# The strip copies of branch B's values: 16 DMAs of 512 KB in the second head group instead of 32 of 256 KB over both

## The chip, the core and the metric

One NeuronCore of a Trainium2 chip runs the whole kernel. Its engines are TensorE (PE, with its weight loads as PEld), VectorE (DVE), ScalarE (ACT), GpSimd (POOL) and SyncE (SP); each takes its instructions strictly in the order of its own list and waits for others by semaphores. SP does nothing but issue DMAs; ACT and POOL issue some as well. The metric is the time of one execution in microseconds, as the median of several runs. The kernel before takes 2136.32 us (2136.04 to 2136.45 in three runs).

## The reference

One encoder layer on two sequences, 512 and 1024 tokens of width 1024, in float32. Branch A is grouped-query attention (8 query heads on 2 key/value heads), branch B is a neighbourhood attention with 8 heads on a token grid 64 wide; both are gated, merged and projected, and a squared-ReLU MLP follows.

```python
z = xn @ w_in
qa, ka, va, qb, kb, vb, ga, gb = jnp.split(z, idx, axis=-1)
...
o_a = _gqa_attention(qa, ka, va)
o_b = _neighbourhood_attention(qb, kb, vb, rpb)   # 8 rows x 16 columns around each token
merged = jax.nn.sigmoid(ga) * (o_a @ w_proj_a) + jax.nn.sigmoid(gb) * (o_b @ w_proj_b)
h = x + merged @ w_out
h = h + jnp.square(jax.nn.relu(rmsnorm(h) @ w_mlp_up)) @ w_mlp_down
```

The values vb of branch B are what the change is about: 1024 tokens x 8 heads x 64 numbers in the longer sequence.

## The kernel before

The two sequences ("trunks") go through `run` one after the other, the short one (512 tokens, `NB` = 1, names with 0) first, the long one (1024 tokens, `NB` = 2, names with 1) second. The MLP of both follows. Every float32 product is made of three matmuls on a high and a low part: `split` (lines 197 to 208) lets ACT cut the high part of a loaded weight tile (L199) and DVE the low part in two halves (L206). Loaded weights pass through three shared buffers (`rawp`), so a load also waits until the load three before it has been cut.

For each trunk `run` does this:

- **Twice, for the head groups g = 0 and 1 (line 538 on):** first the projections of a group, tile by tile of 128 tokens: the heads of branch A (`zs`), and, two tiles behind, the values of branch B for four of the eight heads (`values`, tiles `zvs`, weights `w_vs` from `raw_vs`). Each value tile is split into its high and low part side by side, 128 numbers a head, and written by ACT into the DRAM tensor `vd` (tokens x 8 heads x 128, L652). Then branch A's attention of the group: eight units in the long trunk (`units`, four heads by two blocks of 512 queries), each with eight rounds of transposes, high and low part (`pths`, `ptls`) and products; the gate projection of the branch fills PE's gaps. ACT writes each unit's result (`oads`) and each gate tile (`zgs`) to DRAM.
- **Branch B (line 918 on):** the query and key projection of two heads (`qkproj`: queries `pqbs`, L992 and L994; keys `pkbs`, L1013 and L1015), then units (h, j) of a head h and a strip j of 16 columns: scores (`sbs`), bias (`bms` from `rects`), softmax (`pbs`), a turn through DRAM (`tbs`, `bhs`), and the product with the strip of values `vss` (`obs`). The gate projection of branch B (weights `raw_gs1_3328_c`, c = 0 to 7) fills the gaps.

A strip j needs the values of 32 columns, and neighbouring strips overlap. In the long trunk the kernel therefore first copies `vd` inside DRAM into four strip stores `vst[0..3]` (L808, `vsts` in the profile), rows of a strip standing in the order in which `prep_v` (L950) then loads them for one head, 256 KB for a head and a strip. One copy takes every fourth grid row (index a) of one strip j: a source pattern of 4 x 32 runs and a target of 128 runs. Before the change each run holds the four heads of one group (2 KB), so a copy is 256 KB and there are 16 of them in each group's branch A, two at each unit. The short trunk has no strip stores; it loads straight from `vd` (L956).

The order of each engine's instructions is not the order of the source. A scheduler orders the whole program by its own estimates of when data will be there, and gives the DMAs of SP and ACT eight completion semaphores in turn: a DMA waits until the DMA that had its semaphore before is complete. So a copy in SP's list may wait for a gate or output write of ACT that has nothing else to do with it, and everything behind it in SP's list waits too.

Of the kernel before, what the change touches and what calls it, by code (L numbers as in the profile page):

```python
# [22 lines left out]
GRID_W = 64  # L23
# [38 lines left out]
def encoder(ctx: ExitStack, tc: tile.TileContext, xs, outs, w):  # L62
# [21 lines left out]
    def phase(name, bufs=2):  # L84
        return tc.tile_pool(name=name, bufs=bufs, reuse_waits="tile")
# [7 lines left out]
    def mm(name):  # L93
        return pmm.tile([P, 512], F32, tag="mm", name=name)

    def big(name):
        return pbig.tile([P, 1024], F32, tag="big", name=name)
# [73 lines left out]
    def bias_row(r):  # L171
        nc.sync.dma_start(biases[r], shifted[:, :, 7 - r : 23 - r, :])
# [246 lines left out]
    def run(tr, nxt, first):  # L419
        N, x, T, NT, NB = tr.N, tr.x, tr.T, tr.NT, tr.NB  # L420
# [4 lines left out]
        vd = dram.tile([T, 8, P], F32, name=f"vd{N}")  # L425
        vst = [dram.tile([rows // 4, 32, 4, 8, P], F32, name=f"vst{N}_{j}") for j in range(4)] if NB == 2 else None
# [38 lines left out]
        def finish_o(o, n, dst, pool, nm, parts=None):  # L465

            t = pool.tile([HD, 512], F32, tag="ot", name=f"ot_{nm}", bufs=1)
            if len(o.shape) == 3:

                tv = t[:, : 2 * n].rearrange("p (i q) -> p i q", i=2)  # L470
                nc.scalar.activation(tv, o[HD:P], AF.Copy)
                nc.vector.tensor_tensor(tv, o[0:HD], tv, op=ALU.add)  # L472
                o = tv[:, 1]
            else:
                nc.scalar.activation(t[:, :n], o[HD:P, :n], AF.Copy)
            if parts is not None:
                hi, lo, ps = parts
                b = pool.tile([P, n], F32, tag="os", name=f"os_{nm}", bufs=2)[ps, :n]
                nc.vector.tensor_tensor(b, o[0:HD, :n], t[:, :n], op=ALU.add)
                nc.scalar.activation(hi, b, AF.Copy)  # L480
                nc.vector.tensor_tensor(lo, b, hi.bitcast(F32), op=ALU.subtract)
                return
            b = pool.tile([HD, n], F32, tag="os", name=f"os_{nm}", bufs=2)
            nc.vector.tensor_tensor(b[:, :n], o[0:HD, :n], t[:, :n], op=ALU.add)
            put(dst, b[:, :n])
# [39 lines left out]
        def load_v(g, alloc, pin=False, hold=None):  # L525
            return load_cols(win, 1792 + 256 * g, 256, f"v{N}_{g}", alloc, pin, hold)

        early = {}
        for g in range(2):
# [230 lines left out]
            with phase(f"phA{N}_{g}") as ph:  # L760
                units = [(h, qb) for h in range(4) for qb in range(NB)]
                PP = {}

                def s_tile(u, j):
                    h, qb = u
                    nm = f"{N}_{g}_{h}_{qb}_{j}"
                    q0 = (qb * 4 + j) * P
                    lhs = qT[h % 2][:, h // 2, q0 : q0 + P]
                    s = big(f"s{nm}")[:, :T]
                    for kb in range(NB):  # L770
                        ks = slice(kb * 512, kb * 512 + 512)
                        nc.tensor.matmul(s[:, ks], lhs, kT[:, 0, ks], start=True, stop=False)
                        nc.tensor.matmul(s[:, ks], lhs, kT[:, 1, ks], start=False, stop=True)  # L773
                    nm_ = sml.tile([P, 1], F32, tag="nm", name=f"nm{nm}")
                    nc.vector.tensor_reduce(nm_, s, axis=AX.X, op=ALU.max, negate=True)  # L775
                    p = ph.tile([P, T], F32, tag="P", name=f"p{nm}", bufs=8)
                    l = sml.tile([P, 1], F32, tag="l", name=f"l{nm}")
                    nc.scalar.activation(p, s, AF.Exp, bias=nm_, accum_out=l)  # L778
                    rl = sml.tile([P, 1], F32, tag="rl", name=f"rl{nm}")
                    nc.vector.reciprocal(rl, l)  # L780
                    nc.gpsimd.tensor_scalar(p, p, rl, 1.0, op0=ALU.mult, op1=ALU.mult)  # L781
                    PP[u, j] = p

                o_of = {}

                def pv(u, kc, hi, lo):
                    h, qb = u
                    if kc == 0:
                        o_of[u] = mm(f"o{N}_{g}_{h}_{qb}")
                    o = o_of[u]  # L790
                    nc.tensor.matmul(o, vhl[:, kc, :], hi, start=(kc == 0), stop=False)
                    nc.tensor.matmul(o, vhl[:, kc, :], lo, start=False, stop=(kc == NT - 1))
                    if kc == NT - 1:
                        r0 = (g * 4 + h) * HD
                        finish_o(o, 512, oad[r0 : r0 + HD, qb * 512 : qb * 512 + 512], ph, f"A{N}_{g}_{h}_{qb}")

                for j in range(4):
                    s_tile(units[0], j)
                    fill.pull(2)
                queue = []  # L800
                LAG = 2
                for ui, u in enumerate(units):
                    h, qb = u
                    if NB == 2:
                        hs = slice(4 * g, 4 * g + 4)
                        for a in range(2 * (ui % 2), 2 * (ui % 2) + 2):
                            c0 = (0, 8, 24, 32)[ui // 2]
                            nc.sync.dma_start(  # L808
                                vst[ui // 2][:, :, a, hs, :].rearrange("k c h d -> k c (h d)"),
                                vd[:, hs, :].rearrange("(k a c) h d -> a k c (h d)", a=4, c=GRID_W)[a, :, c0 : c0 + 32],  # L810
                            )
                    if first:
                        bias_row(g * 4 + ui)
                        if g == 0 and ui == 1:
                            early["a"] = load_a(1)
                        if g == 0 and ui == 2:
                            early["v"] = load_v(1, slot)
                    nxt_u = units[ui + 1] if ui + 1 < len(units) else None
                    sdone = 0
                    for kc in range(NT):  # L820
                        pt = mm(f"pT{N}_{g}_{h}_{qb}_{kc}")
                        for j in range(4):
                            nc.tensor.transpose(  # L823
                                pt[:, j * P : (j + 1) * P], PP[u, j][:, kc * P : (kc + 1) * P], ident
                            )
                        hi = ph.tile([P, 512], F32R, tag="pth", name=f"pth{N}_{g}_{h}_{qb}_{kc}", bufs=3)
                        lo = ph.tile([P, 512], F32R, tag="ptl", name=f"ptl{N}_{g}_{h}_{qb}_{kc}", bufs=3)
                        nc.scalar.activation(hi, pt, AF.Copy)  # L828
                        nc.vector.tensor_tensor(lo, pt, hi.bitcast(F32), op=ALU.subtract)  # L829
                        queue.append((u, kc, hi, lo))  # L830
                        if nxt_u is not None:
                            while sdone < 4 and kc >= ((0, 1, 3, 4) if NB == 2 else (0, 0, 1, 2))[sdone]:
                                s_tile(nxt_u, sdone)
                                sdone += 1

                        fill.pull(1 if NB == 1 or kc % 4 < 3 else 0)
                        if len(queue) > LAG:
                            pv(*queue.pop(0))
                fill.drain()
                for item in queue:  # L840
                    pv(*item)
# [80 lines left out]
        with phase(f"phB{N}") as ph:  # L922
# [268 lines left out]
            for i in range(n + 4 - NB):  # L1191
# [9 lines left out]
                if i < n:  # L1201
# [4 lines left out]
                    h, j = units[i]  # L1206
# [702 lines left out]
    for i, tr in enumerate(trunks):  # L1909
        run(tr, trunks[i + 1] if i + 1 < len(trunks) else None, i == 0)  # L1910
# [66 lines left out]
```

## Time and profile before

| | us |
|---|---|
| median of three runs | 2136.32 (2136.04 to 2136.45) |
| the profiled execution | 2136.87 |
| its span, first to last instruction | 2135.0 |
| PE busy / PEld busy | 2099.9 / 1840.2 |
| DVE / ACT / POOL busy | 1483.2 / 1146.3 / 362.0 |
| PE's granted clock, mean over the span | 0.997 |
| copies of the first set, first to last issue | 452.2 to 586.1 |
| copies of the second set, first to last issue | 655.5 to 791.2 |

Columns of rows below: in a timeline, start and length in us, engine, line, operation, output<-inputs, shapes, count, and in brackets the idle time of the engine before it with what ended it. "SPq" and "ACTq" are DMA issues; their length is that of the issue, not of the transfer. Buffer numbers are left out of names, so `vsts<-vds` stands for all copies. In the list of waits the numbers are the total, the count and the longest. Times in the windows and timelines are counted from the span's first instruction. The long trunk's first branch A ends near 581, the second group's projections near 655, its branch A near 782, and branch B follows.

### The profile page before, as it was taken

The page shows a single profiled execution, that of the slowest core. Times are in us where ns is not written, and L with a number is a line of the kernel's source. Part 1 is how long each engine was busy: PE and PEld are TensorE (multiplying, and loading weights), DVE is VectorE, ACT ScalarE, POOL GpSimd, SP SyncE. Part 2 cuts the span into 40 slices and gives each one's busy share as a digit, 9 for nine tenths or more (in the row PEclk, how much of TensorE's full clock was granted, in tenths as well). Part 3 has the DMA queues.
Part 4 walks back from the last instruction along what each step waited for, and adds up shares of the span by engine and source line. Part 5 has one row for each costly group of instructions (what it writes and reads, how often), then busy time and mean ns, then how long its engine had stood idle before and what let it go on. Part 6 is the DMA issues. An engine that isn't in the chain of part 4 may idle for free.

```text
span 2135.0 us, 31762 instructions
## 1 busy us (share of the span) xinstructions
PE 2099.9 (98%) x10871; PEld 1840.2 (86%) x10871; DVE 1483.2 (69%) x2793; ACT 1146.3 (54%) x2487; POOL 362.0 (17%) x446
## 2 busy tenths in 40 slices
PE   9999999999989999999999999999999999999998
PEld 8888778988888888888888899999999988888887
DVE  6665786767647756787882877778777777759563
ACT  6664653767556645555531556556655643434352
POOL 2232310323233314442101200003000000000000
PEclk9999999999999999999999999999999999999999
DMA  6437557520133038876472666578445799688561
GB/s 192 133 99 212 148 165 254 184 89 29 59 111 107 25 97 245 244 219 196 153 246 103 203 196 193 162 249 210 158 146 158 259 351 344 215 276 282 166 203 64
DMA packets 340072, 381.31 MB, mean 179 GB/s; under 512 B 30911, under 2 KB 267079, under 8 KB 339911
## 3 DMA queue, kind: packets, MB, share of 16 engines
q1 hardware_dynamic: 301687, 313.99, 46.9%
q10 hardware_dynamic: 31072, 45.11, 6.0%
q0 software_dynamic: 7152, 20.19, 3.5%
q8 instruction: 86, 1.41, 0.3%
q14 instruction: 75, 0.61, 0.1%
HBM read 282.68 MB, written 105.71 MB: 182 GB/s over the span
## 4 chain that ended last, share of the span: by engine, by line
PE 53%; DVE 1%; issue 0%; ACT 0%; POOLq 0%; POOL 0%; ACTq 0%; DVEq 0%
PE dn L212 20%; PE ua L212 6%; PE ud L212 6%; PE uc L212 6%; PE ops L212 4%; PE ub L212 3%; PE ppbs L212 2%; PE ppas L212 2%; PE dnf L212 2%; PE pt L353 0%; PE obs L212 0%; PE gpss L212 0%; PE sbs L212 0%; PE ptbs L1126 0%; DVE A L1452 0%
## 5 line engine op out<-in xcount | busy, mean ns | idle before, releaser
L212 PE MATMUL dn<-wd,ah 128*128 128x512 f32 x1248 | 384.3, 389 | 0.0
L212 PEld LDWEIGHTS dn<-wd,ah 128*128 128x128 f32 x1248 | 234.2, 188 | 48.7
L212 PE MATMUL dn<-wd,al 128*128 128x512 f32 x624 | 242.8, 389 | 0.0
L1451 ACT ACTIVATE ah<-ar 128x512 fp32r<-128x512 f32 x168 | 104.4, 628 | 206.0 <-PE dn L212 186.7
L212 PE MATMUL gpss<-xs_0h,w_gs 128*128 128x512 f32 x512 | 188.7, 402 | 0.8 <-DVE ot_Bs L472 0.4
L1452 DVE TENSOR_TENSOR al<-ar,ah 128x512 fp32r<-128x512 f32 x168 | 114.4, 687 | 75.5 <-ACT ah L1451 67.9
L212 PE MATMUL ud<-B,A 128*128 128x384 f32 x768 | 143.6, 334 | 0.7 <-DVE c L1569 0.7
L212 PE MATMUL uc<-B,A 128*128 128x384 f32 x768 | 143.7, 334 | 0.0
L212 PE MATMUL ua<-B,A 128*128 128x384 f32 x768 | 138.8, 334 | 0.0
L212 PEld LDWEIGHTS dn<-wd,al 128*128 128x128 f32 x624 | 117.1, 188 | 24.2
L781 POOL TENSOR_SCALAR ps<-ps,rls 128x1024 f32<-128x1024 f32 (+1 forms) x96 | 96.8, 1010 | 226.4 <-DVE rls L780 201.0
L212 PEld LDWEIGHTS ud<-B,A 128*128 128x128 f32 x768 | 133.9, 188 | 1.1 <-DVE c L1569 1.1
L212 PEld LDWEIGHTS uc<-B,A 128*128 128x128 f32 x768 | 134.1, 188 | 0.2 <-ACT A L1451 0.2
L212 PEld LDWEIGHTS ua<-B,A 128*128 128x128 f32 x768 | 133.7, 188 | 0.2
L829 DVE TENSOR_TENSOR ptls<-pTs,pths 128x512 fp32r<-128x512 f32 x160 | 107.7, 686 | 37.3 <-ACT pths L828 36.3
L828 ACT ACTIVATE pths<-pTs 128x512 fp32r<-128x512 f32 x160 | 94.0, 597 | 73.4 <-PE pTs L823 71.3
L212 PE MATMUL ops<-wh_os,mgs 128*128 128x512 f32 x384 | 119.4, 390 | 0.0
L775 DVE TENSOR_REDUCE nms<-ss 128x1 f32<-128x1024 f32 (+1 forms) x96 | 99.9, 1041 | 25.6 <-PE ss L773 25.1
L212 PEld LDWEIGHTS gpss<-xs_0h,w_gs 128*128 128x128 f32 x512 | 96.3, 189 | 18.9 <-DVE w_gs L206 0.7
L778 ACT ACTIVATE ps<-ss,nms 128x1024 f32<-128x1024 f32 (+1 forms) x96 | 93.2, 972 | 23.4 <-DVE nms L775 20.6
L180 POOL TENSOR_TENSOR rs_f<-ms_f,mhalf 128x1 f32<-128x1 f32 x6 | 4.0, 667 | 590.7 <-DVE ms_f L176 590.7
L823 PEld LDWEIGHTS pTs<-ident,ps 128*128 128x128 f32 x640 | 77.7, 140 | 28.6 <-POOL ps L781 4.3
(287 smaller groups left out, 5152.4 us busy)
## 6 DMA issues: line engine op xcount, KB each, us to landing
ar<-ud SPq DMA_DIRECT2D x120, 512.0 KB
br<-in_w_mlp_down_dram SPq DMA_DIRECT2D x72, 512.0 KB
rawu<-in_w_mlp_up_dram SPq DMA_DIRECT2D x64, 512.0 KB
ud<-c ACTq DMA_DIRECT2D x128, 192.0 KB
raw_gs<-in_w_in_dram SPq DMA_DIRECT2D x32, 512.0 KB
ud<-cs SPq DMA_DIRECT2D x64, 192.0 KB
tbs<-pbs SPq DMA_DIRECT2D x24, 384.0 KB
bhs<-tbs SPq DMA_DIRECT2D x24, 384.0 KB
```

Of the source, the lines that this page charges most:

```text
L180: nc.gpsimd.tensor_tensor(r[:, :n], m[:, :n], mhalf[:, :n], op=ALU.pow)
L212: op = nc.tensor.matmul(out, a, b, **kw)
L775: nc.vector.tensor_reduce(nm_, s, axis=AX.X, op=ALU.max, negate=True)
L778: nc.scalar.activation(p, s, AF.Exp, bias=nm_, accum_out=l)
L781: nc.gpsimd.tensor_scalar(p, p, rl, 1.0, op0=ALU.mult, op1=ALU.mult)
L823: nc.tensor.transpose(pt[:, j * P : (j + 1) * P], PP[u, j][:, kc * P : (kc + 1) * P], ident)
L828: nc.scalar.activation(hi, pt, AF.Copy)
L829: nc.vector.tensor_tensor(lo, pt, hi.bitcast(F32), op=ALU.subtract)
L1451: nc.scalar.activation(hi, src, AF.Copy)
L1452: nc.vector.tensor_tensor(lo, src, hi.bitcast(F32), op=ALU.subtract)
```

## The change

The copies are issued in the second group's branch A alone, two at each unit as before, and each now takes all eight heads.

```diff
-                    if NB == 2:
-                        hs = slice(4 * g, 4 * g + 4)
+                    if NB == 2 and g == 1:
                         for a in range(2 * (ui % 2), 2 * (ui % 2) + 2):
                             c0 = (0, 8, 24, 32)[ui // 2]
                             nc.sync.dma_start(
-                                vst[ui // 2][:, :, a, hs, :].rearrange("k c h d -> k c (h d)"),
-                                vd[:, hs, :].rearrange("(k a c) h d -> a k c (h d)", a=4, c=GRID_W)[a, :, c0 : c0 + 32],
+                                vst[ui // 2][:, :, a].rearrange("k c h d -> k c (h d)"),
+                                vd.rearrange("(k a c) h d -> a k c (h d)", a=4, c=GRID_W)[a, :, c0 : c0 + 32],
                             )
```

Thirty-two copies of 256 KB become sixteen of 512 KB; the bytes are the same. The strips of heads 0 to 3 now depend on the second group's copies too. The scheduler orders the program anew, and three places of its lists differ in what follows. (The new file is one line shorter, so lines behind 804 count one less. Numbers at the end of a name are buffers.)

**SP, from the loads for the second group's projections on.** `rawkvs` are weights of that group's branch A, `raw_vs` its value weights, `rts` rotary tables, `raw_gs_2304` gate weights. Before:

```order
L510 DMA rawkvs_1_7022<-in_w_in_dram 128x8x64 x2
L808 DMA vsts_0_4661<-vds_4660 128x1x512 x4
L808 DMA vsts_1_4662<-vds_4660 128x1x512 x4
L808 DMA vsts_2_4663<-vds_4660 128x1x512 x4
L808 DMA vsts_3_4664<-vds_4660 128x1x512 x4
L245 DMA raw_vs_1_0_7031<-in_w_in_dram 128x4x256
L245 DMA raw_vs_1_4_7038<-in_w_in_dram 128x4x256
L708 DMA rts_1_0_7047<-in_rope_dram 128x128
```

After:

```order
L510 DMA rawkvs_1_7006<-in_w_in_dram 128x8x64 x2
L245 DMA raw_vs_1_0_7015<-in_w_in_dram 128x4x256
L245 DMA raw_vs_1_4_7022<-in_w_in_dram 128x4x256
L245 DMA raw_gs_2304_4_0_7603<-in_w_in_dram 128x8x128
L708 DMA rts_1_0_7031<-in_rope_dram 128x128
```

The sixteen copies of the first set stood between the two kinds of weights and are gone; the value weights follow at once. On ACT their two cuts (`wh_vs`, L199) moved with them, from behind the squares of the third tile (`sqs_1_2`) to ahead of those of the first.

**SP, at the second group's copies and the start of branch B.** `rects` are bias rectangles, `raw_gs_3328` the gate weights of branch B, `raw_bqs_1` and `raw_bks_1` the query and key weights of the second pair of heads. Before; the four strip loads of head 0 (`vss_0`, L950) stand seven rows above this piece, ahead of the second set:

```order
L245 DMA raw_gs_3328_0_0_9252<-in_w_in_dram 128x8x128
L808 DMA vsts_0_4661<-vds_4660 128x1x512 x4
L808 DMA vsts_1_4662<-vds_4660 128x1x512 x4
L808 DMA vsts_2_4663<-vds_4660 128x1x512 x4
L808 DMA vsts_3_4664<-vds_4660 128x1x512 x4
L942 DMA rects_0_9233<-biases 128x768
L245 DMA raw_gs_3328_1_0_9395<-in_w_in_dram 128x8x128
L942 DMA rects_1_9434<-biases 128x768
L1255 DMA zgs_1_4666<-sgs_3328_0_0_9454 128x512
L245 DMA raw_gs_3328_2_0_9540<-in_w_in_dram 128x8x128
L245 DMA raw_bqs_1_0_9592<-in_w_in_dram 128x8x128
L245 DMA raw_bks_1_0_9595<-in_w_in_dram 128x8x128
```

After:

```order
L807 DMA vsts_0_4661<-vds_4660 128x1x1024 x4
L807 DMA vsts_1_4662<-vds_4660 128x1x1024 x4
L807 DMA vsts_2_4663<-vds_4660 128x1x1024 x4
L807 DMA vsts_3_4664<-vds_4660 128x1x1024 x4
L941 DMA rects_0_9217<-biases 128x768
L949 DMA vss_0_9219<-vsts_0_4661 128x4x128
L949 DMA vss_0_9219<-vsts_1_4662 128x4x128
L949 DMA vss_0_9219<-vsts_2_4663 128x4x128
L949 DMA vss_0_9219<-vsts_3_4664 128x4x128
L245 DMA raw_gs_3328_1_0_9379<-in_w_in_dram 128x8x128
L941 DMA rects_1_9418<-biases 128x768
L245 DMA raw_gs_3328_2_0_9524<-in_w_in_dram 128x8x128
```

The strip loads of head 0 now stand behind all sixteen copies, and the gate weights of columns 1 and 2 behind the strip loads. The semaphores tie the copies to other DMAs: copies 3, 4, 7, 9 and 11 (counted 1 to 16) wait for output writes (`oads`) of units 2, 5, 6, 7 and 8 of this group; copies 5, 8 and 10 for gate writes (`zgs`), 10 for the last of the group; copies 6 and 12 to 16 for the copies 3 to 8. The strip load of strip 0 waits for copy 10, that of strip 1 for 11, of strip 2 for 12, of strip 3 for 13 to 16.

**ACT, at the start of branch B.** `oads_4667<-os_As_1_3_1` is the last output write of branch A, `qBs` and `kBs` the query and key parts of the first pair of heads, by blocks of 512 tokens (`pqbs_0_0` the first, `pqbs_0_1` the second). Before:

```order
L435 DMA oads_4667<-os_As_1_3_1_9224 64x512
L992 ACTIVATE qBs_0_9258<-pqbs_0_0_9261 64x4x128 x2
L1013 ACTIVATE kBs_0_0_9259<-pkbs_0_0_9296 64x512 x2
L1013 ACTIVATE kBs_0_1_9260<-pkbs_0_0_9296 64x512
L992 ACTIVATE qBs_0_9258<-pqbs_0_1_9328 64x4x128 x2
L1013 ACTIVATE kBs_0_0_9259<-pkbs_0_1_9363 64x512 x2
```

After:

```order
L435 DMA oads_4667<-os_As_1_3_1_9208 64x512
L199 ACTIVATE w_bqs_0_9226<-raw_bqs_0_0_9224 128x1024
L199 ACTIVATE w_bks_0_9232<-raw_bks_0_0_9230 128x1024
L199 ACTIVATE w_gs_3328_0_9238<-raw_gs_3328_0_0_9236 128x1024
L991 ACTIVATE qBs_0_9242<-pqbs_0_0_9245 64x4x128 x2
L1012 ACTIVATE kBs_0_0_9243<-pkbs_0_0_9280 64x512 x2
L1012 ACTIVATE kBs_0_1_9244<-pkbs_0_0_9280 64x512
L199 ACTIVATE w_gs_3328_1_9381<-raw_gs_3328_1_0_9379 128x1024
L199 ACTIVATE w_gs_3328_2_9526<-raw_gs_3328_2_0_9524 128x1024
L991 ACTIVATE qBs_0_9242<-pqbs_0_1_9312 64x4x128 x2
L1012 ACTIVATE kBs_0_0_9243<-pkbs_0_1_9347 64x512 x2
```

The cuts of the first query, key and gate weights came from the midst of branch A to here, and the cuts of gate weights 1 and 2 from behind the first softmax operations to ahead of the second block's queries and keys. DVE's low parts moved along with them.

On PE the only moves are six swaps of a score matmul with the transposes next to it, and the first matmul of the fourth tile's projection, which went some 25 instructions later.

## Prediction

> **What bounds the kernel now.** I read the page first, then PE's waits, the windows, and the timelines of the two stretches that the change touches.
>
> ```profile
> span 2135.0 us, 31762 instructions
> PE 2099.9 (98%) x10871; PEld 1840.2 (86%) x10871; DVE 1483.2 (69%) x2793; ACT 1146.3 (54%) x2487; POOL 362.0 (17%) x446
> GB/s 192 133 99 212 148 165 254 184 89 29 59 111 107 25 97 245 244 219 196 153 246 103 203 196 193 162 249 210 158 146 158 259 351 344 215 276 282 166 203 64
> ```
>
> TensorE is busy for 2099.9 of 2135.0 us, so only some 35 us are waits. A change that moves DMAs can win back a few of these, or add new ones; it removes no matmul. PE's waits, as total, count and longest, name what there is to win:
>
> ```profile
> PE zvs L212 <- ACT wh_vs L199: 5.7, 1, 5.7
> PE sbs L212 <- DVE kBs L1015: 2.3, 2, 1.8
> ```
>
> The longest single wait of the program, 5.7 us, is at the first value matmul (zvs) of the long trunk's second group, for the weights that ACT cuts (wh_vs). The timelines of SP, ACT and PE there show why:
>
> ```profile
> 583.19 3.69 SPq L808 DMA_DIRECT2D vsts<-vds  x4
> 586.99 4.00 SPq L245 DMA_DIRECT2D raw_vs<-in_w_in_dram  x2
> ```
>
> ```profile
> 598.32 1.06 ACT L199 ACTIVATE wh_vs<-raw_vs 128x1024 fp32r<-128x1024 f32 x1 [3.29 <-DMA raw_vs<-in_w_in_dram]
> 599.61 1.06 ACT L199 ACTIVATE wh_vs<-raw_vs 128x1024 fp32r<-128x1024 f32 x1 [0.24 <-DMA raw_vs<-in_w_in_dram]
> ```
>
> ```profile
> 593.35 0.34 PE L212 MATMUL zs<-wghs,xs_0l 128*128 128x384 f32 x1
> 599.43 0.58 PE L212 MATMUL zvs<-wh_vs,xs_0h 128*128 128x256 f32 x1 [5.74 <-ACT wh_vs L199]
> 600.15 0.58 PE L212 MATMUL zvs<-wl_vs,xs_0h 128*128 128x256 f32 x1
> ```
>
> SP issues the value weights only at 586.99, behind the last four copies of the first set, and they land at 598.3, though ACT has been free for 3.3 us. The windows price what follows (columns: stretch, length, busy time of PE, PEld, DVE, ACT and POOL, granted clock, share of the 16 DMA engines, GB/s):
>
> ```profile
> 778.00:781.00 3.00, 3.00 (x17) 2.47 (x16) 1.38 (x2) 1.10 (x2) 0.64 (x1) 1.00 0.26 101
> 598.40:605.20 6.80, 5.33 (x22) 4.82 (x23) 5.28 (x8) 2.67 (x5) 2.96 (x4) 0.50 0.22 64
> ```
>
> From 598.4 to 605.2 the clock is 0.50: the idle stretch is paid a second time. The other row is a stretch in which the copies run with little else: 101 GB/s at a DMA share of 0.26, about four engines of 16. That is why 586.99 became 598.3: four copies of 256 KB at 101 GB/s take 10.4 us, and whatever is queued behind them on those engines waits.
>
> **Part 1, the first group's copies go: a gain.** SP's order after the change has the value weights straight behind the group's other weight loads, and ACT's order has both wh_vs cuts right after the last output write of branch A, ahead of the squares of three tiles. Their buffers are free long before, so the 5.74 us wait goes. So does what it caused: work from 599.4 to 605.2 at half clock, 5.8 us, costs 2.9 us, and a wait of 0.4 us for the low part (wl_vs) that follows in the same stretch is counted in my sum as well. **Gain 9.1 us** (5.74 + 0.44 + 2.9). Bounds: 5.7 if the clock fell for another reason, 9.1 at most. What is late next there? The rotated heads (rrs), which ACT now makes behind 2.1 us of cuts; they have the matmuls of the second and third tile as cover. From here everything in the second group's branch A runs 9.1 us earlier.
>
> **Part 2, cuts moved to the start of branch B: a loss, but a covered one.** The cuts of the query, key and gate weights now stand on ACT behind the last output write of branch A, where before they were done in its midst.
>
> ```profile
> 781.98 0.33 ACTq L435 DMA_DIRECT2D zgs<-sgs  x1
> 782.35 0.59 ACT L475 ACTIVATE ot_As<-os 64x512 f32<-64x512 f32 x1 [0.40 <-PE os L792]
> 783.69 0.46 ACTq L435 DMA_DIRECT2D oads<-os_As  x1
> ```
>
> ```profile
> 782.06 0.39 PE L212 MATMUL pqbs<-xs_0h,w_bqs 128*128 128x512 f32 x1
> 782.29 0.39 PE L212 MATMUL pqbs<-xs_0l,w_bqs 128*128 128x512 f32 x1
> ```
>
> PE starts the query projection at 782.06 now. After the change ACT is free for the cut only at 784.15 (783.69 + 0.46), cuts for 1.05 us, and the low half follows on DVE for 0.86 (both rows below): 786.1, where the second matmul, which needs it, ran at 782.29. That is 3.8 us of waiting, and half as much again of cold clock by the proportion of part 1 (5.74 us of waiting, 2.9 of cold clock) is 1.9. By itself 5.7 us. Part 3 comes later on the same path and swallows it.
>
> **Part 3, sixteen copies of 512 KB in one group: the large term.** Each copy takes one of eight completion counters shared by SP and ACT and waits for the DMA that used that counter before. The waits of SP between 640 and 860 us show it:
>
> ```profile
> SPq L808 <- DMA zgs<-sgs: 112.2, 5, 59.1
> SPq L808 <- DMA oads<-os_As: 14.2, 2, 9.3
> ```
>
> So the copies don't run ahead through the group's 130 us: they are paced by ACT's writes of gates and head outputs. In the changed order copy 9 follows the output write before the last, copy 10 the group's last gate write (zgs, issued at 781.98), copy 11 the last output write, and 12 to 16 only earlier copies. When does the last gate write release SP?
>
> ```profile
> 789.35 3.00 SPq L808 DMA_DIRECT2D vsts<-vds  x4
> 792.47 0.48 SPq L942 DMA_DIRECT2D rects<-biases  x1
> 793.06 2.07 SPq L245 DMA_DIRECT2D raw_gs<-in_w_in_dram  x1
> ```
>
> At 789.35, where copy 13 of before waited for the same write (7.4 us after its issue; the mask's load runs beside it). Four copies of 256 KB are left then. After the change **seven copies of 512 KB** are left, 3.67 MB instead of 1.05.
>
> A 512 KB copy has no row. Its two patterns keep their outer counts, 4 on the source and 128 on the target, and only the run grows from 2 to 4 KB; so I take the rate of the 101 GB/s row: 5.2 us each. Bounds: 1.3 us if all 16 engines took part (four times the rate), 6.2 us if sharing costs a fifth.
>
> By the Trainium skill, DMA: Bandwidth & Descriptors, section "Why a DMA increments its semaphore by 16 and not by 1", a DMA runs on the largest number of engines up to 16 that divides both outer counts, here still 4. The same page's section "Anatomy of one DMA" gives 2.0 us plus bytes at 436 GB/s, an estimate of 1.2 us of moving per copy; by that the sum would be the first rival's below. The share of 0.26 speaks against it here.
>
> What waits for them: all four strip loads of head 0 (vss) now read what these copies write, and the last of them stands in SP's queue behind copies 13 to 16. Behind it stand the gate weights of columns 1 and 2, and on ACT the cuts of these two now stand *ahead* of the second half of the query and key projection, which the first score matmul of branch B needs. Before, ACT had this:
>
> ```profile
> 804.02 1.19 ACT L1013 ACTIVATE kBs<-pkbs 64x512 fp32r<-64x512 f32 x2 [3.31 <-PE pkbs L212]
> ```
>
> ```profile
> 799.20 0.88 DVE L994 SCALAR_TENSOR_TENSOR qBs<-pqbs,qBs 64x128 fp32r<-64x128 f32 x4 [2.10 <-ACT qBs L992]
> 800.74 0.92 DVE L994 SCALAR_TENSOR_TENSOR qBs<-pqbs,qBs 64x128 fp32r<-64x128 f32 x4 [0.66 <-ACT qBs L992]
> 805.24 1.38 DVE L1015 TENSOR_TENSOR kBs<-pkbs,kBs 64x512 fp32r<-64x512 f32 x2 [3.58 <-ACT kBs L1013]
> ```
>
> ```profile
> 806.68 0.80 PE L212 MATMUL sbs<-kBs,qBs 128*128 128x384 f32 x3 [0.48 <-DVE kBs L1015]
> ```
>
> The path step by step, in the changed kernel's time:
> - Copy 10 issued: 789.35 - 9.1 = 780.25.
> - Seven copies: 36.3 us, and 2.0 us from issue to landing (the row pair below): 818.5.
> - Last strip load, gate weights 1, bias rectangle and gate weights 2 (256 + 512 + 384 + 512 KB) at 351 GB/s, the best slice of the page: 4.8 us, and 2.0 to landing: 825.3.
> - ACT cuts gate weights 2, 1.05; DVE's two low halves, 2 x 0.86: 828.0.
> - Query halves, 799.20 to 801.66 before: 2.5; key halves: ACT 1.19, DVE 1.38, with some 0.9 overlapped: **832.2**.
>
> ```profile
> 767.83 0.33 ACTq L435 DMA_DIRECT2D zgs<-sgs  x1
> 769.86 0.58 SPq L808 DMA_DIRECT2D vsts<-vds  x1
> ```
>
> ```profile
> L199 ACT ACTIVATE w_gs<-raw_gs 128x1024 fp32r<-128x1024 f32 x2 | 2.1, 1051 | 0.0
> L206 DVE TENSOR_TENSOR w_gs<-raw_gs,w_gs 128x512 fp32r<-128x512 f32 x4 | 3.3, 857 | 0.8 <-ACT w_gs L199 0.8
> ```
>
> The score matmul that ran at 806.7 runs at 832.2: 25.5 us later, the gain of part 1 already taken off. PE stands idle there for some 29 us (from 803.3, 806.7 - 9.1 + 5.7) with nothing else in its order, and restarts with a cold clock: by the row of part 1, 5.8 us at half, 2.9 us. I add 3.2, a little over it, as this wait is longer. **Net +28.7 us.** By the Trainium skill, TensorE: Matmul & The Clock Gate, section "What's actually happening", one busy window of about 3.4 us lifts the throttle; the restart would then cost 1.7 us, and the sum be 27.2. The 6.8 us of the row decide for me.
>
> Other moves cost nothing by these covers: score matmuls swapped with transposes in branch A (bounds -0.4 to +0.4 us each, the small waits of such places), merge operands (zas) asked for earlier, and the odd head's key copies on POOL behind four bias additions; they have the four units of head 0 as cover, 1 or 2 us if that is gone.
>
> **The sum.** The profiled execution took 2136.87 us, 1.87 around its span and 0.55 over the median of 2136.32. 2136.3 + 28.7 = **2165.0 us** for the median.
>
> **Rivals.**
> - *The copies drain in time.* If they use all engines, 1.3 us each, the chain ends at 805.0, PE gets there at 803.3, and the net is -1.7 us plus up to 1.7 of cold clock: about 2135. Below some 1.0 us a copy the chain is no longer late; there the net is -9.1 + 5.7 = -3.4, 2132.9. For it: 16 issues fewer and runs of twice the length. Against it: the share of 0.26.
> - *Eight engines, 2.6 us each.* The chain ends at 814.1: +7.4 + 2.9, 2146.6. Nothing in the rows points there.
> - *A second wait behind the first.* SP's queue then holds a weight load that waits for DVE ahead of the first softmax stores; if the first output matmul of branch B waits as well, 5 to 12 us more: about 2174.
>
> **How the numbers follow.** Forecast (2155 to 2172) 0.78; first rival 0.10, second 0.04, third 0.08. Within the forecast: 5 us less if the last gate write lands as fast as the earlier one (2.0 us), 3 less without a cold clock, 6 more at 6.2 us a copy. Range 2150 to 2177. Faster or slower means by over 0.2% (4.3 us), about what can be told from no change: faster 0.03, same 0.08, slower 0.89.
>
> **What would show it.** Right: no wait at zvs in the second group and clock 1.00 there; the copies at a DMA share near 0.25 for some 36 us after branch A; gate weights 1 issued some 38 us after copy 10; a PE wait of 25 to 35 us at sbs, put down to kBs. Wrong: copies on all engines; copies 4 to 9 issued much earlier than the writes that pace them; a different ACT operation ahead of the query halves.

## The result, and the profile after

| | before | changed |
|---|---|---|
| median, us (lowest to highest) | 2136.18 (2135.86 to 2136.45) | 2168.45 (2166.51 to 2170.15) |
| the profiled execution, us | 2136.87 | 2166.51 |
| its span, us | 2135.0 | 2164.6 |

The changed kernel is slower by a factor of 1.0151 (95% interval 1.0133 to 1.0168), 32.3 us between the medians. Its profiled execution is the shortest of its four, 29.6 us longer in span than the one before; the rows below explain these 29.6 us.

The page of the changed kernel, and under it its list of PE's waits (total, count, longest):

```profile
span 2164.6 us, 31745 instructions
PE 2100.9 (97%) x10871; PEld 1841.5 (85%) x10871; DVE 1481.8 (68%) x2793; ACT 1148.1 (53%) x2487; POOL 364.0 (17%) x446
```

```profile
PE sbs L212 <- ACT kBs L1012: 32.4, 1, 32.4
PE pqbs L212 <- ACT w_bqs L199: 3.1, 1, 3.1
```

PE is busy for about as long as before (2100.9 against 2099.9 us): no work was added, and 28.6 of the 29.6 us are waiting. The 5.7 us wait at zvs is gone from the list; two waits at the start of branch B have come. SP's timeline shows what holds them:

```profile
782.96 19.38 SPq L807 DMA_DIRECT2D vsts<-vds  x7
802.45 4.68 SPq L941 DMA_DIRECT2D rects<-biases  x1
807.17 13.65 SPq L949 DMA_DIRECT2D vss<-vsts  x4
820.92 0.52 SPq L245 DMA_DIRECT2D raw_gs<-in_w_in_dram  x1
821.48 1.42 SPq L941 DMA_DIRECT2D rects<-biases  x1
823.00 0.38 SPq L245 DMA_DIRECT2D raw_gs<-in_w_in_dram  x1
```

Seven copies are issued from 782.96 on, when the last gate write lets the tenth go. Even their issue stretches over 19 us, and the gate weights follow 38.0 us later. ACT's and PE's timelines carry it on:

```profile
826.35 1.06 ACT L199 ACTIVATE w_gs<-raw_gs 128x1024 fp32r<-128x1024 f32 x1 [33.88 <-DMA raw_gs<-in_w_in_dram]
829.27 1.06 ACT L199 ACTIVATE w_gs<-raw_gs 128x1024 fp32r<-128x1024 f32 x1 [1.87 <-DMA raw_gs<-in_w_in_dram]
830.35 0.59 ACT L991 ACTIVATE qBs<-pqbs 64x512 fp32r<-64x512 f32 x1
```

```profile
834.46 0.69 PE L212 MATMUL sbs<-kBs,qBs 128*128 128x384 f32 x1 [32.35 <-ACT kBs L1012]
```

ACT stood 33.88 us in front of a cut of gate weights, and the query halves (qBs) that PE needed stood behind it in ACT's order. The windows of the changed kernel (stretch, length, busy PE, PEld, DVE, ACT, POOL, granted clock, DMA share, GB/s), first while the seven copies run, then behind the two waits, and last the stretch that was at half clock before:

```profile
784.00:807.00 23.00, 18.11 (x80) 14.64 (x79) 3.85 (x11) 2.75 (x5) 0.00 (x0) 1.00 0.25 101
```

```profile
776.70:779.50 2.80, 2.80 (x7) 2.17 (x8) 2.80 (x5) 1.83 (x2) 0.00 (x0) 0.50 0.61 190
834.50:840.90 6.40, 5.67 (x14) 4.40 (x15) 4.66 (x11) 2.89 (x6) 1.77 (x3) 0.50 1.16 287
598.40:605.20 6.80, 6.80 (x50) 6.80 (x49) 4.36 (x11) 4.13 (x19) 1.67 (x3) 1.00 0.15 52
```

The copies move 101 GB/s at a quarter of the DMA engines, as before. Where PE starts again after these two waits it runs at half clock, for 2.8 and 6.4 us, and half of that is lost. From 598.4 to 605.2 the clock is now full.

### The profile page after: what moved, and what is told of

The parts are those of the page before. It is cut to its first block, busy times and chain, and to the rows that moved or that the text cites. A ratio compares the mean times of both kernels' runs of the same rounds, so it can differ in the third digit from the quotient of the medians.

```text
span 2164.6 us, 31745 instructions
## 1 busy us (share of the span) xinstructions
PE 2100.9 (97%) x10871; PEld 1841.5 (85%) x10871; DVE 1481.8 (68%) x2793; ACT 1148.1 (53%) x2487; POOL 364.0 (17%) x446
## 4 chain that ended last, share of the span: by engine, by line
PE 52%; DVE 1%; issue 0%; ACT 0%; POOLq 0%; POOL 0%; ACTq 0%; DVEq 0%
PE dn L212 19%; PE ua L212 6%; PE ud L212 6%; PE uc L212 6%; PE ops L212 4%; PE ub L212 3%; PE ppbs L212 2%; PE ppas L212 2%; PE dnf L212 2%; PE pt L353 0%; PE obs L212 0%; PE gpss L212 0%; PE sbs L212 0%; PE ptbs L1125 0%; DVE A L1451 0%
```

## The experiments

The theory: time is lost only as the copies that stand behind the last gate write are many and slow. Each takes its bytes at 101 GB/s, because its pattern has 4 as the outer count. The rivals: the rate of a DRAM-to-DRAM copy does not depend on the pattern; the size of one copy hurts; the pacing by ACT's writes hurts whatever the rate; the gain in the first group came from elsewhere.

### half: the same orders, half the bytes

```diff
-vst[ui // 2][:, :, a].rearrange("k c h d -> k c (h d)"),
-vd.rearrange("(k a c) h d -> a k c (h d)", a=4, c=GRID_W)[a, :, c0 : c0 + 32],
+vst[ui // 2][:, :, a, 4:8].rearrange("k c h d -> k c (h d)"),
+vd[:, 4:8].rearrange("(k a c) h d -> a k c (h d)", a=4, c=GRID_W)[a, :, c0 : c0 + 32],
...
-vst[j][:, :, :, h, :].rearrange("k c a d -> (c a) k d")
+vst[j][:, :, :, 4 + h % 4, :].rearrange("k c a d -> (c a) k d")
```

> The changed kernel with copies of 256 KB: the sixteen copies carry heads 4 to 7 only, and the strips of heads 0 to 3 are loaded from those of heads 4 to 7. Every engine's order is that of the changed kernel. Theory (seven copies stand ahead of the last strip load, and each takes its bytes at about 101 GB/s): 2.6 us a copy instead of 5.2, so the chain after the last gate write is 18 us shorter; the wait at the first score matmul of branch B falls from 32.4 to about 14 us, and the time from 2168.5 to about 2150 (2145 to 2152, the lower end if the last gate write also lands sooner). Rival A (the wait is for the gate write that paces the copies, or for their number, not their bytes): no change, 2167 to 2170. Rival B (a second wait behind the first fills what is won): 2160 or more.

Measured: 2140.57 us, ratio to before 1.0019 (1.0010 to 1.0028). The direction is the theory's, the size is not: 28 us less, where 18 were forecast. SP's timeline and PE's waits of this run:

```profile
781.17 2.53 SPq L807 DMA_DIRECT2D vsts<-vds  x4
783.82 1.71 SPq L941 DMA_DIRECT2D rects<-biases  x1
785.57 8.87 SPq L949 DMA_DIRECT2D vss<-vsts  x4
794.53 0.49 SPq L245 DMA_DIRECT2D raw_gs<-in_w_in_dram  x1
```

```profile
PE sbs L212 <- ACT kBs L1012: 4.1, 1, 4.1
PE pqbs L212 <- ACT w_bqs L199: 3.4, 1, 3.4
```

Only four copies are left behind the gate write here, not seven: the scheduler tied the semaphores differently although every engine's order is the same (perhaps because it expects a smaller copy to be done sooner; the runs don't show why). Four copies of 2.6 us are 10.4 us, and the gate weights are issued 13.4 us after the first of them. So the rule fits with the number of copies that this kernel really leaves behind; the expectation had carried the seven over. Rival B falls, and so does the part of A by which the pacing alone makes the wait. Number and bytes went down together here, so the run does not part them cleanly; but four copies of 5.2 us would be 20.8 us, more than the 13.4 that all of it took.

### wide and tiny: the pattern, and the floor

```diff
-vst[ui // 2][:, :, a].rearrange("k c h d -> k c (h d)"),
-vd.rearrange("(k a c) h d -> a k c (h d)", a=4, c=GRID_W)[a, :, c0 : c0 + 32],
+vst[ui // 2][:, :, a].rearrange("k c h d -> c k (h d)"),
+vd.rearrange("(k a c) h d -> a c k (h d)", a=4, c=GRID_W)[a, c0 : c0 + 32],
```

In tiny the pattern is the old one, with `4:5` in the place of `4:8` in the diff of half, and all strips are loaded from head 4.

> The changed kernel with the same sixteen copies of 512 KB, their patterns turned so that the outer dimension is the 32 grid columns on both sides instead of 4 and 128. Theory (the outer count of 4 holds a copy to four of the 16 engines): about 1.3 us a copy, a DMA share of 0.8 or more while they run, the seven copies done in some 10 us, no wait over 5 us at the first score matmul. The scheduler also moves the cuts of the query weights back into branch A here, so the 3.1 us wait at the query projection goes as well: 2127 us (2124 to 2133). Rival A (a copy from DRAM to DRAM runs at about 100 GB/s whatever its pattern): the long wait stays, 2160 to 2166. Rival B (eight engines): 2140 to 2146.

> The changed kernel with copies of 64 KB in the old pattern (4 outside): only head 4 is copied, and all strips are loaded from it. Every engine's order is that of the run wide. Theory: 0.65 us a copy on four engines, so the copies are out of the way, and this is the floor for wide: 2127 us (2124 to 2131), within 3 us of wide. If wide is much longer than this, the copies themselves still cost there; if both stay near 2168, the bytes of the copies are not what is waited for.

Measured: wide 2127.47 us, ratio to before 0.9957 (0.9942 to 0.9972); tiny 2126.83, 0.9954 (0.9939 to 0.9969). SP's row with all sixteen copies of wide, and a window in which they run with few other DMAs:

```profile
646.18 63.30 SPq L807 DMA_DIRECT2D vsts<-vds  x16
```

```profile
658.00:662.00 4.00, 4.00 (x22) 3.24 (x21) 2.65 (x5) 4.00 (x8) 0.72 (x2) 1.00 1.03 394
```

The same bytes, the same 4 KB runs: 394 GB/s at a share of 1.03, where the old order of the dimensions gave 101 at 0.25. This is the best stretch; from 650 to 660 it is 332 GB/s at 1.01. So the share is four times the old one, and the rate three to four times. (The share is a mean over the 16 engines; the trace does not tell them apart.) The rule of the Trainium skill weighed in the prediction (DMA: Bandwidth & Descriptors, "Why a DMA increments its semaphore by 16 and not by 1") agrees at both points: 4 engines for an outer count of 4, 16 for 32.

With tiny, an eighth of the bytes in the old pattern, the time is the same within the spread of either, so in wide the copies cost nothing any more. But the rate is not all that changed. The scheduler ties none of the sixteen to the last gate write here, nor in tiny: all are issued between 646 and 710, while the changed kernel issues the last seven from 782.96 on. The expected seven copies behind the gate write, done in 10 us, never came about, and how much of the gain is rate and how much is place these two runs do not tell. **wide beats both kernels**, by 9.1 us against the kernel before on its chip (2136.53).

### before_wide, wide_g0, wide_g1: where the first group's 9 us come from

The kernel before, in both groups (before_wide), for g == 0 alone (wide_g0) and for g == 1 alone (wide_g1):

```diff
-vst[ui // 2][:, :, a, hs, :].rearrange("k c h d -> k c (h d)"),
-vd[:, hs, :].rearrange("(k a c) h d -> a k c (h d)", a=4, c=GRID_W)[a, :, c0 : c0 + 32],
+vst[ui // 2][:, :, a, hs, :].rearrange("k c h d -> c k (h d)"),
+vd[:, hs, :].rearrange("(k a c) h d -> a c k (h d)", a=4, c=GRID_W)[a, c0 : c0 + 32],
```

> The kernel before, with its 32 copies of 256 KB in both groups, their patterns turned to 32 outside as in wide. Theory: the first set's last four copies take 2.6 us together instead of 10.4, the value weights behind them land some 8 us sooner, the 5.7 us wait at the first value matmul of the second group and the half clock behind it go: 2127 us (2125 to 2131). Rival (that wait has another cause, or the copies' rate does not depend on the pattern): 2135 to 2137.

> The kernel before with the turned pattern (32 outside) for the first group's sixteen copies alone; the second group's copies keep the old pattern and their order. Theory (all of the 9 us come from the value weights that queue behind the first set): no wait at the first value matmul of the second group, full clock there, 2127.5 us (2125.5 to 2129.5), as in the run before_wide. Rival (part of the 9 us came from the second group, for example from strip loads that land sooner): 2129.5 to 2134.

> The mirror of wide_g0: the turned pattern for the second group's copies alone. Theory (at branch B of the kernel before, PE waited only 0.5 us at the first scores, so faster copies have nothing to win there): the 5.7 us wait and the half clock stay, 2135.5 us (2134 to 2137). Rival of wide_g0: 2129 to 2134.

| run | median, us | ratio to before (95% interval) |
|---|---|---|
| before_wide | 2127.53 | 0.9957 (0.9941 to 0.9974) |
| wide_g0 | 2127.81 | 0.9957 (0.9941 to 0.9973) |
| wide_g1 | 2135.43 | 0.9994 (0.9984 to 1.0003) |

All three times came out as forecast. The whole gain comes from the first group: with the new pattern in its sixteen copies alone the 9 us are there. Faster copies in the second group alone give nothing, since before PE waited 0.5 us there. The way to the gain was another than forecast, though. Expected were four last copies that take 2.6 us in place of 10.4, and value weights that land some 8 us sooner. SP's timeline of wide_g0:

```profile
452.42 13.77 SPq L808 DMA_DIRECT2D vsts<-vds  x16
485.78 51.50 SPq L245 DMA_DIRECT2D raw_vs<-in_w_in_dram  x2
```

All sixteen are issued within 14 us, where before they took 134.65 us (452.22 to 586.87): none is held up by ACT's late writes any more. The value weights are issued 50 to 100 us sooner, and ACT cuts them at 583.44 without a wait for a DMA. before_wide shows the same. So it is shown that the 9 us go when the value weights no longer stand behind late copies; whether the rate alone would have done it, with the copies as late as before, is not. The longest waits of wide_g0 and wide_g1, one row of each list:

```profile
PE ss L772 <- ACT kTs L626: 2.5, 3, 1.2
```

```profile
PE zvs L212 <- ACT wh_vs L199: 6.1, 1, 6.1
```

In wide_g0 no single wait over 2 us is left in this list; in wide_g1 the wait for the value weights stays (6.1 us).

### last7_wide and first9_wide: rate and place apart

The edit of wide, in last7_wide only where this holds, in first9_wide only where it doesn't:

```diff
+2 * ui + a % 2 >= 9
```

> The changed kernel with the turned pattern (32 outside) for the copies 10 to 16 alone, those behind the last gate write. Every engine's order and every copy's semaphore wait are those of the changed kernel; only the rate of these seven differs. Theory (their rate alone makes the long wait): 1.3 us a copy instead of 5.2, 9 us in all instead of 36, so gate weights 1 are issued some 12 us after copy 10 (38 in the changed kernel), and the wait at the first scores falls from 32.4 to 1 to 5 us; the 3.1 us wait at the query projection and its cold clock stay: 2137 us (2132 to 2142). Rival A (the pacing by ACT's writes is the cause, whatever the rate): 2160 or more. Rival B (the copies 1 to 9 are still draining in front of them): 2145 to 2155.

> The mirror: the turned pattern for the copies 1 to 9, the old one for 10 to 16. Every engine's order is that of the changed kernel, but the scheduler ties the copies to other semaphores: copy 16 waits for the gate write before the last (some 760 us), no copy for the last one. Seven copies still run on four engines, 5.2 us each. Theory (a slow copy costs nothing if it is not left behind the last gate write): all copies done by some 780 us, no long wait at the first scores (under 4 us), the 3.1 us wait at the query projection stays: 2133 us (2130 to 2140). Rival (slow copies cost as such): 2145 to 2168.

Measured: last7_wide 2143.93 us, ratio 1.0032 (1.0020 to 1.0043); first9_wide 2130.86, 0.9973 (0.9961 to 0.9985). In last7_wide orders and semaphores are those of the changed kernel, and the rate of seven copies alone takes 24.5 us off. SP's timeline, a window while the seven run, and PE's waits:

```profile
782.71 5.14 SPq L807 DMA_DIRECT2D vsts<-vds  x7
...
798.63 0.45 SPq L245 DMA_DIRECT2D raw_gs<-in_w_in_dram  x1
```

```profile
788.00:796.00 8.00, 8.00 (x37) 6.64 (x36) 2.06 (x3) 1.78 (x3) 0.00 (x0) 1.00 0.99 307
```

```profile
PE sbs L212 <- ACT kBs L1012: 9.5, 1, 9.5
PE pqbs L212 <- ACT w_bqs L199: 3.1, 1, 3.1
```

The gate weights are issued 15.9 us behind the tenth copy (12 forecast, 38.0 in the changed kernel). The DMA share is 0.99, but the window, in which bias rectangles and strip loads run among the copies, has 307 GB/s, not 394; at that rate a copy is 1.7 us. So the wait is 9.5 us and not 1 to 5, and the time 2 us above the range that was forecast. Rival A falls. Rival B does not quite: the tenth copy goes at 782.71, as in the changed kernel, but from 779 to 783, before it is under way, the share is 0.25 to 0.29 at 82 to 99 GB/s, so an earlier copy of the old pattern is still running. What that adds to the 9.5 us was not tried.

first9_wide is the other half: seven copies run in the old pattern, but the scheduler ties none of them to the last gate write. A window while some of them run, and two rows of SP, the last copy and the first strip loads behind it:

```profile
664.00:672.00 8.00, 8.00 (x49) 6.79 (x48) 6.32 (x10) 4.64 (x9) 2.25 (x2) 1.00 0.25 103
```

```profile
764.92 0.58 SPq L807 DMA_DIRECT2D vsts<-vds  x1
...
778.25 1.03 SPq L949 DMA_DIRECT2D vss<-vsts  x2
```

They are as slow as ever (103 GB/s at 0.25), and cost nothing: the last is issued at 764.92, 18 us ahead of the changed kernel's tenth, and PE's wait at the first scores is 0.5 us. The 3.1 us wait at the query projection is left; with its cold clock it is more than the 3.4 us by which this run is above wide. **A slow copy is not what hurts, but a slow copy left behind the last gate write with SP's loads in its queue.**

### pieces: 32 copies of 256 KB in the second group

```diff
-nc.sync.dma_start(
-    vst[ui // 2][:, :, a].rearrange("k c h d -> k c (h d)"),
-    vd.rearrange("(k a c) h d -> a k c (h d)", a=4, c=GRID_W)[a, :, c0 : c0 + 32],
-)
+for hs in (slice(0, 4), slice(4, 8)):
+    nc.sync.dma_start(
+        vst[ui // 2][:, :, a, hs, :].rearrange("k c h d -> k c (h d)"), vd[:, hs, :].rearrange("(k a c) h d -> a k c (h d)", a=4, c=GRID_W)[a, :, c0 : c0 + 32],
+    )
```

> The changed kernel with its sixteen copies cut into 32 of 256 KB, all in the second group's branch A, old pattern: the place is changed, the size is that of before. By the scheduler's semaphores the 25th copy is the one that waits for the last gate write, so eight copies of 2.6 us (2.1 MB) stand behind it, where the changed kernel had seven of 5.2 us (3.7 MB). Theory (bytes behind the last gate write at 101 GB/s): 21 us of copies, first scores some 16 us sooner than in the changed kernel, a wait there of 14 to 20 us: 2150 us (2144 to 2156). Rival A (the size of one copy is what hurts): 2127 to 2137. Rival B (all bytes being in one group hurts, however they are cut): 2165 to 2172.

Measured: 2176.28 us, ratio 1.0183 (1.0167 to 1.0199): a miss by 20 us over the range. SP's and ACT's timelines:

```profile
791.78 10.60 SPq L808 DMA_DIRECT2D vsts<-vds  x8
802.49 4.36 SPq L941 DMA_DIRECT2D rects<-biases  x1
806.89 6.84 SPq L949 DMA_DIRECT2D vss<-vsts  x4
813.84 2.15 SPq L245 DMA_DIRECT2D raw_bqs<-in_w_in_dram  x1
```

```profile
820.89 1.06 ACT L199 ACTIVATE w_bqs<-raw_bqs 128x1024 fp32r<-128x1024 f32 x1 [35.47 <-DMA raw_bqs<-in_w_in_dram]
```

The chain of copies is what was forecast: eight of them, and the last strip load of head 0 is through SP 22.0 us after the first of the eight was issued. What failed is who stands behind it. In this order the query weights (raw_bqs) do too, which branch B needs first of all; the expectation had reckoned with the gate weights alone. PE waits 37.3 us at the query projection. The eight start 8.8 us later than the seven of the changed kernel as well (3.3 us of it is a new wait of PE in the second group's projections). Rival A (the size of one copy) falls: no copy of 512 KB is needed for the harm. Rival B (all bytes in one group) is not parted from the theory, since the order changed too, and its range of 2165 to 2172 lies nearer to what came out.

### pool_queue: the copies from another queue

```diff
-                            nc.sync.dma_start(
+                            nc.gpsimd.dma_start(
```

> The changed kernel with its sixteen copies (512 KB, old pattern, same place) issued from POOL's queue instead of SP's, two after each unit's softmax: they share no semaphore with ACT's gate and output writes, and nothing of SP's stands behind them. The scheduler reorders branch A's scores and transposes around them, so a few us either way belong to that. Theory (a slow copy does harm only as far as the pacing leaves it behind the last gate write, with SP's loads queued after it): the copies are done soon after 780 us, no wait over 6 us at the first scores, 2130 us (2125 to 2138). Rival (the copies' total time on four engines is the limit, or POOL's issue of them delays the softmax): 2145 or more.

Measured: 2149.17 us, ratio 1.0055 (1.0039 to 1.0071). Its list of DMA issues (KB each, median us from issue to landing) and PE's waits in the stretch:

```profile
vsts<-vds POOLq DMA_DIRECT2D x16, 512.0 KB, 8.7
```

```profile
PE ss L772 <- ACT ps L778: 9.3, 11, 2.7
PE os L791 <- ACT pths L827: 2.8, 4, 1.0
PE os L792 <- DVE ptls L828: 1.9, 5, 1.1
PE sbs L212 <- DVE kBs L1014: 0.5, 1, 0.5
```

The copies are still slow, 8.7 us to landing. At the first scores PE waits 0.5 us, as the theory said; but 14 us of small waits have come in branch A, and the time lies in the range of the rival. Whether the other order of scores and transposes makes these waits, or POOL's issue of the copies, was not parted. Inconclusive for the price, in line with the theory at the one place it was for.

### The waits add up

Each run's profiled execution against that of before_wide (2126.89 us), which has none of these waits; cold clock is half of the stretch at 0.50 behind each wait, by the window rows of that run. The rows that aren't above are these, of half, last7_wide and first9_wide:

```profile
776.80:782.80 6.00, 6.00 (x14) 4.75 (x15) 3.65 (x6) 1.81 (x2) 0.00 (x0) 0.50 0.18 53
807.80:813.60 5.80, 5.08 (x12) 4.00 (x13) 4.67 (x11) 2.89 (x6) 1.37 (x3) 0.50 1.20 290
```

```profile
777.00:780.30 3.30, 3.30 (x8) 2.58 (x9) 3.30 (x6) 1.79 (x2) 0.00 (x0) 0.50 0.52 159
812.20:817.90 5.70, 4.98 (x12) 3.90 (x13) 4.66 (x11) 2.88 (x6) 1.28 (x3) 0.50 1.20 290
```

```profile
776.65:779.75 3.10, 3.10 (x7) 2.38 (x8) 3.10 (x4) 1.79 (x2) 2.23 (x2) 0.50 0.43 149
```

| kernel | zvs | pqbs | sbs | cold clock | 2126.9 + sum | profiled |
|---|---|---|---|---|---|---|
| before | 5.7 + 0.4 | - | - | 2.9 | 2135.9 | 2136.87 |
| changed | - | 3.1 | 32.4 | 1.4 + 3.2 | 2167.0 | 2166.51 |
| half | - | 3.4 | 4.1 | 3.0 + 2.9 | 2140.3 | 2140.14 |
| last7_wide | - | 3.1 | 9.5 | 1.7 + 2.9 | 2144.1 | 2143.93 |
| first9_wide | - | 3.1 | - | 1.6 | 2131.6 | 2130.74 |

Within 1 us in all five: three waits and the clock behind them are nearly the whole difference between these kernels. The two others with an order of their own don't close so well. In pieces the waits (37.3 and 3.6 us) and the cold clock behind them (6.0 us at half clock near 615, 3.6 behind the long wait) give 2172.6, of 2176.05; in pool_queue the 14 us of waits give 2140.9, of 2149.4.

## Why the prediction was right, by its own steps

| step | predicted | measured |
|---|---|---|
| 1: gain at zvs | 9.1 us | 9.2 us (wide_g0 2127.81 against 2137.0 on its chip) |
| 2: wait at the query projection, cold clock | 3.8 and 1.9 us | 3.1 and 1.4 us |
| 3: copies behind the last gate write | 7 | 7 |
| tenth copy issued | 780.25 | 782.96 |
| from there to gate weights 1 | 38 us | 38.0 us |
| gate weights 2 landed | 825.3 | 829.27 |
| PE at the first scores, and the scores | 803.3, 832.2 | 802.1, 834.46 |
| cold clock behind it | 3.2 us | 3.2 us |

- **Part 1 was right in cause and size.** wide_g0 and wide_g1 show it apart from the second group's copies: the wait and its cold clock go when the value weights are no longer queued behind late copies, and stay otherwise.
- **Part 2 was right in kind, a little too dear.** In the changed kernel part 3 does swallow it: had PE not waited these 3.1 us, it would have reached the scores sooner and waited there for longer. Where part 3 is gone (first9_wide), it is what is left.
- **Part 3 was right**: the number of copies, their rate, the two gate-weight cuts in ACT's order in front of the query halves. last7_wide and first9_wide show rate and place, each by itself. Three of its terms were mis-sized. The tenth copy came 2.7 us late: the gate write that releases it took 9.6 us from its issue (773.35 to 782.96), where 7.4 had been taken over from before. And the loads behind the strips took longer to land, 8.3 us from the issue of gate weights 1 to the landing of gate weights 2, where 6.8 had been reckoned. From there to the scores it took 5.2 us, where 6.9 had been reckoned. So the scores come 2.3 us later than forecast, and with PE's earlier arrival that is the wait of 32.4 us where 29 were forecast. The profiled execution is 29.6 us longer than the one before, 28.7 were forecast: that the sum is so close is in part luck, as the terms erred both ways. The median is 3.5 us over 2165.0, but 1.9 of this is its distance from the profiled execution, which no trace explains.
- **The rivals.** "The copies drain in time" needed all 16 engines. last7_wide is nearest to its condition, seven copies behind the last gate write with all engines in use, and it takes 2143.93 us with a wait of 9.5, not the 2135 of this rival; wide (2127.5) is no test of it, as no copy is left behind the gate write there. The 1.2 us a copy that the prediction took from the Trainium skill (DMA: Bandwidth & Descriptors, "Anatomy of one DMA") is stated there for DMAs issued from GpSimd, which these are not. In pool_queue, which does issue them there, mostly two at a time, the median from issue to landing is 8.7 us. "Eight engines" has no row. No second wait stood behind the first: the list has none over 0.7 us between there and the next pair of heads.
- **The clock.** After the long wait half clock lasted 6.4 us of work, after the two others of that place (half, last7_wide) 5.8 and 5.7. The choice of the 6.8 us row was right at this place. Behind the 3.1 us waits it was 2.8 to 3.3 us, but behind the 3.4 us wait of half 6.0. The one window of the Trainium skill that the prediction weighed (TensorE: Matmul & The Clock Gate, "What's actually happening") is near the short stretches and half of the long ones. The Trainium skill also says there that the window runs freely. The clock record of these traces agrees: with the idle time counted in, the stretches at half clock behind these waits are whole multiples of 3.413 us: 6.83 in the kernel before, 3.41 and 34.13 in the changed one, 6.83 twice in half, 3.41 and 10.24 in last7_wide, 3.41 in first9_wide. Behind the waits at the query projection it was one such window where PE started again up to 0.6 us into it (776.68, clock down from 776.09, in the changed kernel) and two where it started 0.7 us into it (776.77, from 776.05, in half). So 0.3 us more of waiting cost another 3.4 us of half clock. That the start's place in the window decides is read from these few cases and was not varied by itself.

What stays open: why the changed kernel's four runs spread over 3.6 us where those of before spread over 0.6, and what the copies still running at the last gate write add to the long wait.

## What to carry to other kernels

Read the share of DMA engines while a transfer runs alone: 0.25 is the work of four engines out of 16, and here exchanging two dimensions of the pattern, at no cost, made it three to four times as fast. Before moving slow transfers, look at what releases the last of them and what is queued behind: 3.7 MB at 101 GB/s cost 32 us of PE behind the last gate write, and nothing where the last copy was issued 18 us sooner. And count the transfers behind that point anew in every variant, and name everything queued behind them: a scheduler that sees other sizes ties other semaphores and orders other loads behind them, which threw off two of the forecasts here (half and pieces) and brought three others to their number by another way (wide, before_wide, wide_g0).

## What the runs showed of the hardware

- **Copies on four engines seem to delay a small write of another queue.** The last gate write (256 KB, ACT's queue) was issued at 773.35 in the changed kernel and at 773.27 in first9_wide:

```profile
773.35 0.33 ACTq L435 DMA_DIRECT2D zgs<-sgs  x1
```

```profile
773.27 0.33 ACTq L435 DMA_DIRECT2D zgs<-sgs  x1
```

SP goes on behind it at 782.96 in the one, with three copies of 512 KB issued from 757.3 on, and at 778.25 in the other, where the last was issued at 764.92: 9.6 against 5.0 us. In last7_wide, with three copies of the old pattern ahead as in the changed kernel, it is 9.1 (773.62 to 782.71). That they are the cause was not tried by itself.

- **SP's issue itself is held up.** A copy's issue takes 0.58 us alone; of the seven the longest took 6.7 us, and all together 19.38 us. With the turned pattern seven issues take 5.14 us.
- **DRAM-to-DRAM copies in the turned pattern** moved 394 GB/s in the best 4 us of wide and 332 from 650 to 660; in last7_wide, with strip loads among them, it was 307. The share was near 1.0 each time. Why the rates differ was not tried.
- **The granted clock changes on a grid of 3.413 us** in these traces: every stretch at half clock that ends within a trace is 1, 2, 3, 10 or 11 times as long. The waits that they belong to stand under "The clock" above.
